# A one-core hybrid block: the context's decayed keys are made a pair ahead, and nine loads of the modulation's gate move behind the pairs

## The chip, the cores and the metric

The kernel runs on one core of one Trainium2 chip. TensorE (PE in the profile, with its weight loads as PEld), VectorE (DVE), ScalarE (ACT), GpSimd (POOL) and SyncE (SP, which here only starts loads) each work through a queue of their own in order, and wait for each other through semaphores. The metric is the time of one execution on the device in microseconds; less is better. Three runs of the kernel before gave 1631.05, 1633.28 and 1633.43 us, so the median is 1633.28 us.

## The reference

One block works on 256 tokens `x` of width 2048 and 256 context tokens `ctx`. Both are normalised and modulated by `c` and `c_ctx` through `w_ada`, and multiplied with one wide matrix `w_in`. Its columns feed a windowed attention, a gated linear recurrence (HGRN2) that runs in both directions, and two merge gates. The two branches go through `w_o_hgrn` and `w_o_attn`, are merged, and go through `w_out`; the result is scaled by a gate, which is the third part of the modulation, and added to `x`.

Two pieces matter here. The first is the state which the recurrence starts from. The context's tokens give it, with one forget gate f per token and channel, and keys k = 1 - f:

```python
def hgrn2_final_state(k, v, logf):
    G = jnp.cumsum(logf, axis=2)
    w = k.astype(jnp.float32) * jnp.exp(G[:, :, -1:, :] - G)
    return jnp.einsum('bhsk,bhsv->bhkv', w, v.astype(jnp.float32))

s_f = hgrn2_final_state(ck_f, cv_h, cg_f)
s_b = hgrn2_final_state(flip_t(ck_b), flip_t(cv_h), flip_t(cg_b))
```

So w, the decayed key of a context token, is its key times the product of all the forget gates behind it (ahead of it for the other direction). The second is the modulation's gate:

```python
mod = jax.nn.silu(c) @ w_ada[l] + b_ada[l]
shift, scale, gate = jnp.split(mod[:, None, :], 3, axis=-1)
h = h + gate * merge_and_project(...)
```

## The kernel before, in words

A matrix product in float32 is made of three products of rounded halves: each weight chunk (128 partitions x 1024 values, 512 KB, tile `raw`, four buffers) is loaded by SP's queue (L66), rounded on ACT to `wh` (L76), and the rest is left on DVE as `wl` (L77), three buffers each. PE then multiplies (L83, L84, L85, or L141 and L146 for columns whose two halves share a product). What PE does with one such chunk for 256 tokens is called a unit here; it is half a `STEP`.

The program has four stretches: the modulation with the first projections (to about 130 us), the forget gates and values of all heads (to about 570 us, gates written to DRAM as `F_dr`), the eight pairs of heads of the recurrence (570 to 1066 us), and then the output products with the attention between them.

In the third stretch `pair` is a generator. It issues some work of its own and yields how many `STEP`s of other work PE is to do before its next piece; `weave` takes that other work from `inputs`: output gates, merge gates, attention keys and values, and last the query columns of the next pair (L141, L146). PE's order is this order of writing. On DVE, ACT, POOL and SP the framework's scheduler sets the order when the kernel is built; `high_priority` marks the `wh` and `wl` work as urgent.

A pair's steps, by the names in the profile:

- The gates `F[0]` and `F[1]` (forward and backward; 512 columns for each of two heads, first the 256 tokens, then the 256 context tokens) come back from DRAM through POOL's queue (L1083). `load_forgets` for the next pair is called once four `STEP`s of other work are done. `F0` has two buffers, `F1` one.
- `E`, the decayed keys of the context: POOL writes the ones (L765, L766), DVE runs four scans (L770, L771) which multiply up the gates, and two operations (L774) make (f - 1) times the product. `E` lies in the pair's own tile `X2`.
- `tw`: eight transposes of `E` on PE (L899); ACT copies them to `wT` (L900). `to` (L993) turns the result of the pair before, and `sb` (L915) multiplies `wT` with the context's values.
- `copies` and `grow` (ACT L807 and L810, DVE L880): at levels 1, 2, 4, up to 64 the queries and keys are copied to slots and multiplied by gates; `al` (L834) are the products of those copies, in two sets. The first set has the levels up to 4, the second 8 to 64. Several slots are halves of `F0` and `F1` that are no longer needed: the context half of `F1` holds the queries of level 1, that of `F0` the keys of level 4.
- `own`, then `ob` (L973 to L975): the pair's output. `AT` and a state, both in `X2`, are read there.

Between these, `gates` makes the modulation's gate in 32 chunks: a load of `w_ada` into a `raw` buffer, and two operations on DVE that add it to `acc` (L194, L196). After each eight, four transposes `tqg` and a sum (L202, L204, L206) end a quarter. `with_gates` takes one chunk for every two `STEP`s of other work. What is left is run before `part_a`, the products with `w_o_hgrn` (four blocks of eight units each).

## Time and profile before

| What | Value |
|---|---|
| Median of three runs | 1633.28 us (1631.05 to 1633.43) |
| The profiled execution, its own time | 1626.34 us |
| Its span, first to last instruction | 1624.6 us |
| Mean granted clock of TensorE | 0.993 of full speed |
| Matmuls on PE | 10522, busy 98% of the span |
| DVE busy / ACT busy | 71% / 54% of the span |
| Data moved | 312.76 MB, mean 193 GB/s |

The profiled execution was 6.9 us shorter than the median. A row of a group gives the line, engine, operation, output and inputs, the count after the x, the time it was busy, the mean of one in ns, and then how long the engine had stood idle just before and on what. A row of waits gives who waited on whom, the total in us, how often, and the longest. A row of a stretch gives its bounds, its length, the busy time of each engine with the count of its instructions, the granted clock (1.00 is full speed), the share of the DMA engines and the GB/s. A row of the chain of work gives start, length, and what it was; rows of time order add the shape. A row of transfers gives the count, the KB of one, and the median us from issue to landing.

### The profile page before, as it was taken

What the parts mean: (1) busy time and instruction counts of PE and PEld (TensorE: products, weight loads), DVE (VectorE), ACT (ScalarE), POOL (GpSimd) and SP (SyncE); (2) the same over time, 40 slices, a digit from 0 to 9 for tenths busy, and PEclk for the clock granted to TensorE, in tenths of its full rate; (3) what the DMA queues carried; (4) which work ended last, traced back from release to release, by engine and by line L of the source; (5) the groups of instructions that cost most, each with busy time, mean ns of one, the idle gap of its engine ahead of it and who ended that gap; (6) DMA issues with size and microseconds to landing.
All of it is one profiled execution on the core that took longest, in us unless ns stands there. A gap on an engine that the chain in (4) does not pass through costs nothing.

```text
span 1624.6 us, 26679 instructions
## 1 busy us (share of the span) xinstructions
PE 1584.1 (98%) x10522; PEld 1335.9 (82%) x10522; DVE 1151.7 (71%) x1703; ACT 873.0 (54%) x1343; POOL 84.9 (5%) x183
## 2 busy tenths in 40 slices
PE   7999999999999999999999989999999999999998
PEld 4668888888899987888887877888888888878887
DVE  4449788888877777877878777555567767656764
ACT  4334465656543356645655656443457678744442
POOL 2000000000000010011010010000000000000000
PEclk9999999999999999999999999999999999999999
DMA  9994544444433477665766766455554445467662
GB/s 369 386 368 162 168 124 140 140 142 137 137 124 126 145 262 235 215 211 186 250 218 222 240 202 226 134 178 192 184 179 139 149 130 169 156 220 246 207 199 87
DMA packets 230013, 312.76 MB, mean 193 GB/s; under 512 B 10080, under 2 KB 145664, under 8 KB 228992
## 3 DMA queue, kind: packets, MB, share of 16 engines
q1 hardware_dynamic: 216800, 266.85, 50.3%
q0 software_dynamic: 12368, 43.11, 7.9%
q8 instruction: 82, 1.34, 0.3%
q10 hardware_dynamic: 720, 1.11, 0.2%
q14 instruction: 43, 0.35, 0.1%
HBM read 290.05 MB, written 20.98 MB: 191 GB/s over the span
## 4 chain that ended last, share of the span: by engine, by line
PE 87%; DVE 6%; DMA 3%; issue 2%; ACT 1%; POOL 0%; POOLq 0%; DVEq 0%; ACTq 0%
PE pj L83 13%; PE pj L84 13%; PE pj L85 13%; PE pj L141 6%; PE pj L630 5%; PE pm L630 5%; PE pj L146 3%; DMA raw<-in_w_ada_dram 3%; PE pj L633 3%; PE pm L633 3%; PE pj L415 2%; PE pa L311 2%; DVE wl L77 2%; PE pj L705 1%; PE pj L704 1%
## 5 line engine op out<-in xcount | busy, mean ns | idle before, releaser
L77 DVE TENSOR_TENSOR wl<-raw,wh 128x1024 fp32r<-128x1024 f32 x308 | 375.8, 1222 | 187.0 <-ACT wh L76 186.3
L76 ACT ACTIVATE wh<-raw 128x1024 fp32r<-128x1024 f32 x308 | 325.0, 1057 | 300.3 <-PE pj L85 218.5
L83 PE MATMUL pj<-wh,xHL 128*128 128x512 f32 (+1 forms) x832 | 324.4, 395 | 0.3 <-DVE hsum L156 0.3
L84 PE MATMUL pj<-wl,xHL 128*128 128x512 f32 (+1 forms) x832 | 323.2, 389 | 1.3 <-DVE wl L77 1.3
L85 PE MATMUL pj<-wh,xHL 128*128 128x512 f32 (+1 forms) x832 | 322.7, 388 | 0.0
L84 PEld LDWEIGHTS pj<-wl,xHL 128*128 128x128 f32 x832 | 157.8, 190 | 32.6 <-DVE wl L77 2.8
L85 PEld LDWEIGHTS pj<-wh,xHL 128*128 128x128 f32 x832 | 157.6, 189 | 32.4
L83 PEld LDWEIGHTS pj<-wh,xHL 128*128 128x128 f32 x832 | 157.9, 190 | 31.4 <-DVE hsum L156 0.7
L141 PE MATMUL pj<-xHL,wh 128*128 128x512 f32 x512 | 180.9, 395 | 0.0
L146 PE MATMUL pj<-xHL,wl 128*128 128x256 f32 x512 | 140.6, 285 | 0.0
L606 DVE TENSOR_TENSOR wl<-raw,wh 128x1024 fp32r<-128x1024 f32 x76 | 92.8, 1221 | 35.1 <-ACT wh L605 34.9
L605 ACT ACTIVATE wh<-raw 128x1024 fp32r<-128x1024 f32 x76 | 80.3, 1057 | 67.9 <-PE pj L630 22.3
L141 PEld LDWEIGHTS pj<-xHL,wh 128*128 128x128 f32 x512 | 95.0, 188 | 18.6
L605 ACT ACTIVATE wh<-T 128x1024 fp32r<-128x1024 f32 x57 | 60.5, 1061 | 80.9 <-PE pm L630 19.4
L84 PE MATMUL pj<-wl,bH 128*128 128x512 f32 x256 | 100.4, 393 | 0.4 <-DVE wl L77 0.4
L85 PE MATMUL pj<-wh,bL 128*128 128x512 f32 x256 | 99.4, 390 | 0.0
L146 PEld LDWEIGHTS pj<-xHL,wl 128*128 128x128 f32 x512 | 96.7, 189 | 2.5
L83 PE MATMUL pj<-wh,bH 128*128 128x512 f32 x256 | 91.8, 392 | 0.1
L606 DVE TENSOR_TENSOR wl<-T,wh 128x1024 fp32r<-128x1024 f32 x57 | 69.6, 1221 | 22.7 <-ACT wh L605 22.6
L880 DVE TENSOR_TENSOR A<-A,X 128x512 f32<-128x512 f32 x96 | 61.8, 685 | 7.6 <-ACT qk L810 2.4
L196 DVE SCALAR_TENSOR_TENSOR acc<-raw,cg,acc 128x512 f32<-128x512 f32 x60 | 44.8, 747 | 31.0 <-DMA raw<-in_w_ada_dram 30.9
L84 PEld LDWEIGHTS pj<-wl,bH 128*128 128x128 f32 x256 | 48.1, 188 | 10.8 <-DVE wl L77 1.0
(356 smaller groups left out, 2872.0 us busy)
## 6 DMA issues: line engine op xcount, KB each, us to landing
raw<-in_w_in_dram SPq DMA_DIRECT2D x300, 512.0 KB, 3.6
raw<-in_w_ada_dram SPq DMA_DIRECT2D x96, 512.0 KB, 7.6
raw<-in_w_o_hgrn_dram SPq DMA_DIRECT2D x32, 512.0 KB, 3.6
raw<-in_w_o_attn_dram SPq DMA_DIRECT2D x32, 512.0 KB, 4.2
F<-F POOLq DMA_DIRECT2D x29, 512.0 KB, 4.5
raw<-in_w_out_dram SPq DMA_DIRECT2D x28, 512.0 KB, 4.0
v<-vo POOLq DMA_DIRECT2D x8, 512.0 KB, 3.8
X<-in_x_dram SPq DMA_DIRECT2D x2, 1024.0 KB, 7.1
```

The lines of the kernel that those rows point to most:

```text
L76: act.activation(h[:, :n], raw[:, :n], AF.Copy)
L77: dve.tensor_tensor(lo[:, :n], raw[:, :n], h[:, :n].bitcast(F32), op=ALU.subtract)
L83: pe.matmul(o, s[0], m[0], start=first, stop=False)
L84: pe.matmul(o, s[0], m[1], start=False, stop=False)
L85: pe.matmul(o, s[1], m[0], start=False, stop=last)
L141: pe.matmul(banks[i].rearrange("p (a t) -> p a t", a=2), h[:, j, cs_], xHL[:, :, kt, :T], start=kt == 0, stop=kt == KT - 1)
L146: pe.matmul(banks[i][:, :T], lo[:, j, cs_], xH[:, kt, :T], start=False, stop=False)
L605: act.activation(h, src, AF.Copy)
L606: dve.tensor_tensor(lo, src, h.bitcast(F32), op=ALU.subtract)
L630: pe.matmul(m_[z].rearrange("p (z a t) -> p z a t", z=2, a=2), h[:, k, :], mv(k), start=fresh and k == 0, stop=False, skip_group_check=True)
L633: pe.matmul(pairs_of(m_[z][:, :T]), lo[:, k, :], mv(k)[:, 0], start=False, stop=k == 7, skip_group_check=True)
L880: dve.tensor_tensor(av, av, f.unsqueeze(3).to_broadcast([P, 2, n2, b]), op=ALU.mult)
```

## The change

The decayed keys are no longer made in `pair`. A new function `ctx_decay` makes them where `load_forgets` has issued the loads of the next pair's gates. It scans into a scratch tile `e` (tag `sm`, three buffers, shared with other work), and then overwrites the context half of `F[d]` with (f - 1) times `e`. The transposes read that half, and `E` in `X2` is gone. Since level 1's copy goes into the context half of `F1`, `copies(1)` moves behind the transposes, and the transposes move to the front of the pair: no other work is left between the pair before and them, and all 1.5 `STEP`s come behind. For the gate, a chunk is taken for every three `STEP`s and not two; the rest is taken in `part_a`, one chunk for every two units.

```diff
+    def ctx_decay(F):
+        rev = lambda a: bass.AP(a.tensor, a.offset + T - 2, [list(a.ap[0]), [-1, T - 1]])
+        for d in range(2):
+            e = base.tile([P, 512], F32, tag="sm", name="e", bufs=3).rearrange("p (h t) -> p h t", h=2)
+            for i in range(2):
+                if d == 0:
+                    pool.memset(e[:, i, T - 1: T], 1.0)
+                    dve.tensor_tensor_scan(rev(e[:, i, 0: T - 1]), rev(F[0][:, i, T + 1: 512]), zeros[:, : T - 1], 1.0,
+                                           ALU.mult, ALU.add)
+                else:
+                    pool.memset(e[:, i, 0:1], 1.0)
+                    dve.tensor_tensor_scan(e[:, i, 1:T], F[1][:, i, T: 511], zeros[:, : T - 1], 1.0, ALU.mult, ALU.add)
+            dve.scalar_tensor_tensor(F[d][:, :, T:], F[d][:, :, T:], -1.0, e, op0=ALU.add, op1=ALU.mult)
@@ pair
-        E = X2[:, :1024].rearrange("p (d h t) -> p d h t", d=2, h=2)
+        E = [F[d][:, :, T:] for d in range(2)]
-        for i in range(2):
-            pool.memset(E[:, 0, i, T - 1: T], 1.0)
-            pool.memset(E[:, 1, i, 0:1], 1.0)
-            fa = F[0][:, i, T + 1: 512]
-            ea = E[:, 0, i, 0: T - 1]
-            rev = lambda a: bass.AP(a.tensor, a.offset + T - 2, [list(a.ap[0]), [-1, T - 1]])
-            dve.tensor_tensor_scan(rev(ea), rev(fa), zeros[:, : T - 1], 1.0, ALU.mult, ALU.add)
-            dve.tensor_tensor_scan(E[:, 1, i, 1:T], F[1][:, i, T: 511], zeros[:, : T - 1], 1.0, ALU.mult, ALU.add)
-
-        for d in range(2):
-            dve.scalar_tensor_tensor(E[:, d], F[d][:, :, T:512], -1.0, E[:, d], op0=ALU.add, op1=ALU.mult)
...
-        copies(1)
-        yield 0.5
         wT = X2[:, 1024:].rearrange("p (a s) -> p a s", a=8)
         for d in range(2):
             tw = ps.tile([P, 512], F32, tag=alt(), name="tw")
             for i in range(2):
                 for s in range(2):
-                    pe.transpose(tw[:, (2 * i + s) * P: (2 * i + s + 1) * P], E[:, d, i, s * P: (s + 1) * P], ident)
+                    pe.transpose(tw[:, (2 * i + s) * P: (2 * i + s + 1) * P], E[d][:, i, s * P: (s + 1) * P], ident)
             act.activation(wT[:, 4 * d: 4 * d + 4, :], tw.rearrange("p (a b) -> p a b", a=4), AF.Copy)
-        yield 1.0
+        copies(1)
+        yield 1.5
@@ load_forgets
             nc.gpsimd.dma_start(F[d].rearrange("p i t -> p (i t)"), F_dr[d][n])
+        ctx_decay(F)
         return F
@@ with_gates
-            if count[0] >= 2 * STEP:
-                count[0] -= 2 * STEP
+            if count[0] >= 3 * STEP:
+                count[0] -= 3 * STEP
                 next(gate, None)
@@ part_a
-    run(gate)
...
-        by = proj_tok(w_oh, n * 512, b_st, range(2))
+        by = proj_tok_g(w_oh, n * 512, b_st, range(2))
+        for z in range(4):
+            take(gate, 1)
+            for _ in range(2):
+                next(by)
+        by = result(by)
...
     for n in range(4):
         part_a(n)
+    run(gate)
```

The order on three engines, as the kernels are built. First PE, from the end of one pair (`ob`) to the next pair's transposes (`tw`); before:

```order
L975 MATMUL ob<-so,A 128x128
L83 MATMUL pj<-wh,xHL 128x512
L84 MATMUL pj<-wl,xHL 128x512
L85 MATMUL pj<-wh,xHL 128x512
...
L899 MATMUL tw<-cs,X_6051 128x128 x8
```

and now:

```order
L979 MATMUL ob<-so,A 128x128
L902 MATMUL tw<-cs,F_5746 128x128 x4
L902 MATMUL tw<-cs,F_5747 128x128 x4
L83 MATMUL pj<-wh,xHL 128x512
L84 MATMUL pj<-wl,xHL 128x512
```

The unit of twelve matmuls that stood between the two stands behind the transposes now, which read the gates' tiles `F0` and `F1` of the pair.

Second DVE in the first pair, between its first set of `al` and its second; `copy_predicated` keeps a level from that first set, L880 (now L885) is `grow`, `wl` belongs to the units. Before:

```order
L880 TENSOR_TENSOR A<-A,X_5433 128x128x4 x2
L196 SCALAR_TENSOR_TENSOR acc<-raw,cg,acc 128x512
L849 COPY_PREDICATED X_5433<-mk,al 128x4x32
L515 TENSOR_TENSOR sgg<-pj,sgg 128x512
L196 SCALAR_TENSOR_TENSOR acc<-raw,cg,acc 128x512
L849 COPY_PREDICATED X_5433<-mk,al 128x4x32
L880 TENSOR_TENSOR A<-A,X_5433 128x64x8 x2
```

and now:

```order
L196 SCALAR_TENSOR_TENSOR acc<-raw,cg,acc 128x512
L761 SCALAR_TENSOR_TENSOR e<-F_5747,zero 128x255 x2
L854 COPY_PREDICATED X_5445<-mk,al 128x4x32
L885 TENSOR_TENSOR A<-A,X_5445 128x64x8 x2
L77 TENSOR_TENSOR wl<-raw,wh 128x1024
L762 SCALAR_TENSOR_TENSOR F_5747<-F_5747,e 128x2x256
```

The two scans (the listing calls them by the same operation as L762) and the product of the next pair's `F1` stand in this place now, ahead of `grow` and a `wl`.

Third SP, the loads at the end of the pairs and in `part_a`. Before:

```order
L66 DMA raw<-in_w_ada_dram 128x2x512
L66 DMA raw<-in_w_in_dram 128x2x512 x2
L66 DMA raw<-in_w_o_hgrn_dram 128x2x512 x32
L66 DMA raw<-in_w_in_dram 128x2x512 x8
```

and now:

```order
L66 DMA raw<-in_w_in_dram 128x2x512 x3
L66 DMA raw<-in_w_ada_dram 128x2x512 x2
L66 DMA raw<-in_w_o_hgrn_dram 128x2x512 x2
L66 DMA raw<-in_w_ada_dram 128x2x512
...
L66 DMA raw<-in_w_ada_dram 128x2x512
L66 DMA raw<-in_w_o_hgrn_dram 128x2x512 x14
```

Of the 32 loads of `w_ada` that the gate takes, all stood ahead of the first load of `w_o_hgrn`; now 23 do, and nine stand behind it, one after every two loads, up to the eighteenth.

## The prediction

> **What bounds the kernel now.** I read the page's first part, then who PE waited for in the stretch of the eight pairs, then that stretch's busy time and clock, and last the chain of work at two of the waits.

> ```profile
> span 1624.6 us, 26679 instructions
> PE 1584.1 (98%) x10522; PEld 1335.9 (82%) x10522; DVE 1151.7 (71%) x1703; ACT 873.0 (54%) x1343; POOL 84.9 (5%) x183
> ```

> PE is the bound: it is idle for 1624.6 - 1584.1 = 40.5 us of the whole. A change can win only from those, or from time in which PE runs at a lower clock. Stretches of the trace (bounds, length, PE, PEld, DVE, ACT and POOL busy, clock, DMA share, GB/s), the first the pairs, the next four around single stalls, the last `part_a`:

> ```profile
> 570.00:1060.00 490.00, 469.11 (x4344) 396.01 (x4343) 375.58 (x631) 284.72 (x527) 49.22 (x114) 0.98 0.66 216
> 587.00:594.00 7.00, 3.88 (x16) 3.15 (x16) 7.00 (x13) 3.04 (x5) 0.00 (x0) 0.76 0.62 223
> ...
> 826.00:833.00 7.00, 4.61 (x18) 3.45 (x17) 7.00 (x15) 2.74 (x5) 1.58 (x2) 0.76 0.66 221
> 885.00:895.00 10.00, 6.59 (x22) 5.54 (x22) 8.31 (x17) 2.98 (x6) 0.98 (x1) 0.66 0.46 152
> 947.00:956.00 9.00, 5.50 (x21) 4.05 (x20) 7.97 (x17) 4.86 (x8) 1.09 (x2) 0.81 0.62 206
> ...
> 1066.00:1163.00 97.00, 97.00 (x450) 80.53 (x449) 49.68 (x50) 39.80 (x48) 2.34 (x4) 1.00 0.60 196
> ```

> In the pairs PE is idle for 490.0 - 469.1 = 20.9 us. What it waited for there:

> ```profile
> PE tw L899 <- DVE X L774: 16.7, 8, 3.4
> PE pj L84 <- DVE wl L77: 1.3, 1, 1.3
> ```

> The transposes of `E` waiting for DVE's last operation on `E` are 16.7 of the 20.9 us, over eight pairs. And a long stall costs twice: after four of them the clock falls (0.76, 0.76, 0.66 and 0.81 as means of those stretches). The lost clock is (1 - 0.76) x 7 = 1.7, 1.7, 3.4 and 1.7 us, a little of it inside the idle itself. The chain at the second pair shows why DVE is late (start, length, what):

> ```profile
> 643.98 0.60 DVE acc L196
> ...
> 644.64 1.22 DVE wl L77
> 645.86 0.33 DVE hsum L156
> ...
> 646.52 0.60 DVE X L770
> 647.12 0.58 DVE X L771
> ...
> 648.78 0.68 DVE X L774
> 649.50 1.26 PE tw L899 x8
> 650.76 0.23 PE pj L83
> ```

> Four scans and two products run in a row behind the gate's `acc`, a `wl` and `hsum`, and PE has one unit of twelve matmuls at 0.23 us, 2.7 us, as cover.

> **The change part by part.**

> *The transposes' wait, pairs 2 to 8.* The next pair's `F1` is issued when the first `al` set has read the old one:

> ```profile
> 611.50 0.46 PE L834 MATMUL al<-qk 128*32 128x32 f32 x32
> 612.79 0.53 POOL L1083 DMA_DIRECT2D F<-F  x1 [29.50 <-ACT wh L76]
> F<-F POOLq DMA_DIRECT2D x15, 512.0 KB, 5.7
> ```

> It lands at about 612.8 + 5.7 = 618.5, while the pair it is for wants its transposes as soon as `ob` has ended, at 643.9 (just ahead of the chain quoted above). That leaves 25 us for three DVE operations; `F0` has two buffers and comes earlier still. So `E` is there, and without the first pair's stall (3.1 us: 587.9 to 591.0) the gain is 16.7 - 3.1 = 13.6 us. Its bounds are 13.6 and, should DVE be late again, the rivals below.

> *The clock behind these stalls.* Without the first pair, 1.7 + 3.4 + 1.7 = 6.8 us by the rows above, some of it in the idle already counted. I take 6; the bounds are 4 and 7.

> [...]

> *The first pair gets worse.* Here nothing is made ahead: the gates `F0` land just before.

> ```profile
> 584.94 0.25 PE pj L141
> ...
> 587.45 1.26 DVE X L770 x2
> ...
> 590.35 0.61 DVE X L774
> 591.01 1.97 PE tw L899 x8
> ```

> DVE keeps this order (one `acc` of 0.4 us moves behind), so `E` is ready at about 590.5 as before. But PE has no unit left between 585.2 and the transposes; it idles 5.3 us, not 3.1, and the unit comes after. That is 2.7 - 0.5, with a little more at the lower clock: +2.5 us, bounds +2 and +4.

> *DVE's work moves into the pair before.*

> ```profile
> L77 DVE TENSOR_TENSOR wl<-raw,wh 128x1024 fp32r<-128x1024 f32 x123 | 149.9, 1221 | 63.9 <-ACT wh L76 63.4
> L196 DVE SCALAR_TENSOR_TENSOR acc<-raw,cg,acc 128x512 f32<-128x512 f32 x60 | 44.8, 747 | 31.0 <-DMA raw<-in_w_ada_dram 30.9
> L770 DVE TENSOR_TENSOR_SCAN X<-F,zero 128x255 f32<-128x255 f32 x16 | 10.7, 672 | 0.1
> L774 DVE SCALAR_TENSOR_TENSOR X<-F,X 128x512 f32<-128x512 f32 x16 | 10.4, 677 | 0.0
> ```

> Counts and durations stay: per direction two scans and a product, 2 x 0.67 + 0.68 = 2.0 us. The `F0` half now stands near the start of a pair, where 4.0 us have gone; that is room. The `F1` half stands between the first and the second `al` set, in front of `grow` and a `wl`. By the order and these durations DVE gets there some four to six microseconds after the first set's start (an estimate), and `F1` lands 612.8 + 5.7 - 611.5 = 7.0 us after it. So DVE waits 1 to 3 us there, with everything behind it in its queue: the rest of `grow`, from which the second set's copies are made, and the units' `wl`. What they have to spare in the first pair:

> ```profile
> 627.30 0.62 ACT L810 ACTIVATE so<-A 128x512 f32<-128x512 f32 x1
> 630.98 0.65 PE L834 MATMUL al<-so,acc 128*32 128x64 f32 x32
> ```

> The copy ends at 627.9, PE reads it at 631.0: 3.1 us (the least of the eight; the others have up to 6). Against it: 2.0 us of work, about 2 of waiting, 2.6 because PE comes earlier; for it: 4.0 - 2.0 at the pair's start, and the gate. A chunk costs DVE two operations of 0.75 us, and 30.9 us of waiting for its load over 32 chunks, so about 2.5 us; a pair had four and gets under three, so some 3 us. Nearly even: 6.6 against 5, on 3.1 to 6 us to spare. I take 0.4 us for each of seven pairs, +3; the bounds are 0 and 10.

> POOL's queue gets the same 32 small fills as before, ahead of loads that land long before their use: nothing. `copies(1)` moves behind the transposes on ACT, 1 us of PE, while the first `al` set is six units away: nothing.

> *The gate in `part_a`.* There PE never waits (97.00 of 97 us), and DVE, busy 49.7 us, has room for nine chunks' 13.5 us. What is scarce is the four `raw` buffers. Now three loads come in two units, 5.5 us, so a buffer's turn is 4/3 of that, 7.3 us, and must hold the landing, `wh` and `wl`:

> ```profile
> raw<-in_w_o_hgrn_dram SPq DMA_DIRECT2D x24, 512.0 KB, 3.6
> raw<-in_w_ada_dram SPq DMA_DIRECT2D x32, 512.0 KB, 4.3
> raw<-in_w_ada_dram SPq DMA_DIRECT2D x96, 512.0 KB, 7.6
> L76 ACT ACTIVATE wh<-raw 128x1024 fp32r<-128x1024 f32 x128 | 134.8, 1056 | 105.2 <-PE pj L85 61.1 <-PE pj L141 17.5 <-issue 11.2
> GB/s 369 386 368 162 168 124 140 140 142 137 137 124 126 145 262 235 215 211 186 250 218 222 240 202 226 134 178 192 184 179 139 149 130 169 156 220 246 207 199 87
> ```

> The rows are: `part_a` (3.6 us at 196 GB/s), the gate in the pairs (4.3 at 216), and the whole run, most of it in the first slices (7.6 at 369 to 386). With half as much again `part_a` wants about 290 GB/s, so I estimate a landing of 5 to 6 us. 5.3 + 1.06 + 1.22 = 7.6 us, 0.3 over the turn, over eighteen units (49 us): +2; with DVE's queue waiting for a chunk's load now and then I take +3. The bounds are 0 (4.3 us landing, 6.6 in all) and +18 (7.6 us landing, 9.9 in all: 36% of 49 us).

> *The sum.* -13.6 - 6 + 2.5 + 3 + 3 = -11 us. The profiled execution would come from 1626.3 to about 1615. The median of the runs is 6.9 us above that execution, and I take the same difference for the change: 1633.3 - 11 = **1622 us**.

> **The rivals.**

> *DVE becomes the bound inside the pairs.* The stall at `tw` goes, and comes back at the second `al` set or as a wait for `wl`, since DVE waits for `F1` in its queue. For it: DVE was busy 375.6 of 490 us, and its queue is in order. Against it: PE waited for `wl` once, 1.3 us, though `acc` kept DVE waiting 21 times. At 1.5 us more for each of seven pairs, +10, the gain is nearly gone: -1, so 1632; at half of that 1627.

> *The gate's loads starve `part_a`* (the side on which it gets slower). If with nine more loads the transfers land as late as at the start, 7.6 us, a buffer's turn is 9.9 us and PE waits 18 us there: -11 - 3 + 18 = +4, so 1637. It decides from a landing of about 7 us, where the loss is the 14 us won elsewhere. For it: 290 GB/s is three quarters of the highest slice. Against it: the pairs' 216 GB/s cost only 0.7 us of landing more than `part_a`'s 196.

> *The keys are not ready after all* for one reason or another, and the transposes wait without their unit of cover: 16.7 + 7 x 2.7 = 36 us of stalls, 1650 and more. The 25 us speak against it.

> **How the numbers follow.** A measurement of this kernel tells about 0.2%, 3.3 us, from no change. I give my forecast 0.67, DVE as the bound 0.18, the starved `part_a` 0.08, keys not ready 0.04; 0.03 is left for more than the forecast allows. Faster by more than 3.3 us are the forecast, the last case and a third of the second: 0.67 + 0.03 + 0.07 = 0.77. No change is the rest of the second and a part of the third, 0.13. Slower is the remaining 0.10. The forecast's own range goes from all terms at their good ends (-13.6 - 7 + 2 = -19, 1614) to 1628. The range on record is 1612 to 1632: below, small waits of the other 4.2 us may go too; above, it takes in most of the second case.

> **What would show it.** PE's wait at `tw` should be one entry of about 5 us, in the first pair, and its clock low only behind that one. PE's idle time in the pairs should be 10 to 13 us. Any new wait should name `al` on ACT or DVE, or `wl`. DVE should wait for `F` about seven times, 1 to 3 us each, and for `w_ada` less than 30.9 us. In `part_a` the landing should be under 6 us and PE idle under 5. I am wrong if the transposes wait in later pairs, if PE's new waits in the pairs exceed 10 us, or if `part_a` grows by more than 5.

## The result and the profile after

The changed kernel takes 1618.84 us, the kernel before 1633.36 us (medians of four runs each): a ratio of 0.9911, 95% interval 0.989 to 0.9932. Measured again (the run after_again below) it takes 1619.75 us against 1628.36 us, a ratio of 0.9947, 0.9933 to 0.9961. Two executions, one of after_again at 1737.60 us and one of own_cover_late at 3178.83 us, lie far above all others and are left out of the medians and ratios here. The change is faster in both comparisons. Its own time is nearly the same in both; the kernel before was 5 us slower in the first than in the three later jobs, where its 47 runs have medians of 1627.2 to 1628.4 us. Three of the four runs of the kernel before in the first comparison are those that were on record before the change was timed, so the second is the better one; why the kernel before was slower then stays open. The gain is 14.5 us by the first comparison and 8.6 us by the second.

The profiled execution took 1616.09 us. The first part of its page:

```profile
span 1614.3 us, 26652 instructions
PE 1578.8 (98%) x10522; PEld 1331.8 (82%) x10522; DVE 1152.6 (71%) x1703; ACT 869.5 (54%) x1343; POOL 82.3 (5%) x183
```

The work is the same in number. The pairs and the stage behind them, as stretches with the busy time of PE, PEld, DVE, ACT and POOL, the clock, the DMA share and GB/s:

```profile
570.00:1060.00 490.00, 477.01 (x4415) 404.06 (x4414) 372.20 (x625) 285.90 (x539) 50.13 (x115) 0.99 0.66 213
1060.00:1160.00 100.00, 98.24 (x442) 79.52 (x441) 62.24 (x69) 40.05 (x42) 0.58 (x1) 1.00 0.69 223
```

PE is idle for 490.0 - 477.0 = 13.0 us in the pairs, where it was 20.9. The clock lost there, which is PE's busy time in each microsecond times the missing share of the clock, is 2.0 us in sum, where it was 7.5. Behind the pairs PE is idle for 1.8 us, where it never was. What PE waited for in the pairs (us in all, times, the longest):

```profile
PE pj L84 <- DVE wl L77: 3.3, 5, 1.4
PE tw L902 <- DVE F L762: 5.4, 1, 5.4
PE ob L979 <- DVE X L965: 3.3, 2, 1.9
PE pj L146 <- DVE wl L77: 0.8, 2, 0.5
```

The transposes wait once, in the first pair, and the clock falls only behind that wait:

```profile
585.00:598.00 13.00, 7.56 (x30) 6.18 (x29) 11.25 (x21) 6.73 (x12) 0.25 (x4) 0.74 0.56 194
```

The waits for `wl` and at `ob` have grown: 7.4 us together, where there were 1.3 for `wl` and 1.0 for `X` at `ob`. DVE's own waits in the pairs say where they come from:

```profile
DVE acc L196 <- DMA raw<-in_w_ada_dram: 29.6, 15, 5.5
DVE e L761 <- DMA F<-F: 5.7, 6, 1.6
```

DVE waits 5.7 us for the gates in six pairs, and, with nine chunks fewer, still 29.6 us for the loads of `w_ada` (30.9 before). The chain of waits ahead of the first and longer of the two waits at `ob` (1.9 us) shows one such load:

```profile
690.72 7.72 DMA raw<-in_w_ada_dram
...
698.46 0.76 DVE acc L196
...
699.91 1.22 DVE wl L77
701.13 0.79 DVE X L965 x3
...
701.96 0.49 PE ob L979 x2
```

DVE takes its queue in order here. It stands at the add for 5.49 us, until the load has landed, starts it at 698.46 us, and then PE's `wl` (699.91) and the operations on `X` (701.05) come one after another.

In the stage behind the pairs the loads of `w_o_hgrn` land later than before (3.6 us there), and ACT, which never waited for them, does now:

```profile
raw<-in_w_o_hgrn_dram SPq DMA_DIRECT2D x24, 512.0 KB, 4.7
```

```profile
ACT wh L76 <- DMA raw<-in_w_o_hgrn_dram: 23.6, 11, 4.0
```

The pairs' last `ob` starts 15.4 us earlier (1066.1 to 1050.7), and the attention behind `part_a` starts about 10 us earlier. So the pairs won some 15 us in the two profiled executions, and the stage behind them gave 4 to 5 back.

### The profile page after: what moved, and what is told of

Read it like the earlier page. It is cut to its first block, busy times and chain, and to the rows that moved or that the text cites. A ratio compares the mean times of both kernels' runs of the same rounds, so it can differ in the third digit from the quotient of the medians.

```text
span 1614.3 us, 26652 instructions
## 1 busy us (share of the span) xinstructions
PE 1578.8 (98%) x10522; PEld 1331.8 (82%) x10522; DVE 1152.6 (71%) x1703; ACT 869.5 (54%) x1343; POOL 82.3 (5%) x183
## 4 chain that ended last, share of the span: by engine, by line
PE 87%; DMA 5%; DVE 4%; issue 2%; ACT 1%; SPq 0%; POOL 0%; POOLq 0%; DVEq 0%; ACTq 0%
PE pj L84 13%; PE pj L83 13%; PE pj L85 13%; PE pj L141 6%; PE pj L630 5%; PE pm L630 5%; PE pj L146 3%; PE pj L633 3%; PE pm L633 3%; DMA raw<-in_w_ada_dram 2%; DVE wl L77 2%; PE pj L415 2%; PE pa L311 2%; DMA F<-F 1%; PE pj L705 1%
## 5 line engine op out<-in xcount | busy, mean ns | idle before, releaser
L77 DVE TENSOR_TENSOR wl<-raw,wh 128x1024 fp32r<-128x1024 f32 x308 | 375.4, 1221 | 167.4 <-ACT wh L76 166.5
L76 ACT ACTIVATE wh<-raw 128x1024 fp32r<-128x1024 f32 x308 | 324.6, 1056 | 287.5 <-PE pj L85 180.5
L84 PE MATMUL pj<-wl,xHL 128*128 128x512 f32 (+1 forms) x832 | 322.1, 387 | 3.3 <-DVE wl L77 3.3
L83 PE MATMUL pj<-wh,xHL 128*128 128x512 f32 (+1 forms) x832 | 322.2, 392 | 0.0
L85 PE MATMUL pj<-wh,xHL 128*128 128x512 f32 (+1 forms) x832 | 321.2, 386 | 0.0
L84 PEld LDWEIGHTS pj<-wl,xHL 128*128 128x128 f32 x832 | 156.8, 188 | 36.0 <-DVE wl L77 6.7
L85 PEld LDWEIGHTS pj<-wh,xHL 128*128 128x128 f32 x832 | 156.6, 188 | 31.8
L83 PEld LDWEIGHTS pj<-wh,xHL 128*128 128x128 f32 x832 | 156.7, 188 | 30.6 <-ACT sg L211 0.4
L141 PE MATMUL pj<-xHL,wh 128*128 128x512 f32 x512 | 180.9, 395 | 0.0
L141 PEld LDWEIGHTS pj<-xHL,wh 128*128 128x128 f32 x512 | 95.0, 188 | 18.6
L84 PE MATMUL pj<-wl,bH 128*128 128x512 f32 x256 | 100.9, 395 | 2.2 <-DVE wl L77 2.2
L85 PE MATMUL pj<-wh,bL 128*128 128x512 f32 x256 | 99.3, 390 | 0.0
L83 PE MATMUL pj<-wh,bH 128*128 128x512 f32 x256 | 92.0, 393 | 0.1
L606 DVE TENSOR_TENSOR wl<-T,wh 128x1024 fp32r<-128x1024 f32 x57 | 69.6, 1221 | 22.9 <-ACT wh L605 22.9
L196 DVE SCALAR_TENSOR_TENSOR acc<-raw,cg,acc 128x512 f32<-128x512 f32 x60 | 44.9, 748 | 32.9 <-DMA raw<-in_w_ada_dram 32.4
L885 DVE TENSOR_TENSOR A<-A,X 128x512 f32<-128x512 f32 x96 | 61.8, 685 | 4.8 <-ACT so L815 2.4
L84 PEld LDWEIGHTS pj<-wl,bH 128*128 128x128 f32 x256 | 48.1, 188 | 13.8 <-DVE wl L77 4.0
## 6 DMA issues: line engine op xcount, KB each, us to landing
raw<-in_w_in_dram SPq DMA_DIRECT2D x300, 512.0 KB, 3.7
raw<-in_w_ada_dram SPq DMA_DIRECT2D x96, 512.0 KB, 7.8
raw<-in_w_o_hgrn_dram SPq DMA_DIRECT2D x32, 512.0 KB, 4.6
raw<-in_w_o_attn_dram SPq DMA_DIRECT2D x32, 512.0 KB, 4.2
F<-F POOLq DMA_DIRECT2D x29, 512.0 KB, 4.8
raw<-in_w_out_dram SPq DMA_DIRECT2D x28, 512.0 KB, 4.3
v<-vo POOLq DMA_DIRECT2D x8, 512.0 KB, 4.0
```

Source lines behind the costliest of these rows:

```text
L76: act.activation(h[:, :n], raw[:, :n], AF.Copy)
L77: dve.tensor_tensor(lo[:, :n], raw[:, :n], h[:, :n].bitcast(F32), op=ALU.subtract)
L83: pe.matmul(o, s[0], m[0], start=first, stop=False)
L84: pe.matmul(o, s[0], m[1], start=False, stop=False)
L85: pe.matmul(o, s[1], m[0], start=False, stop=last)
L141: pe.matmul(banks[i].rearrange("p (a t) -> p a t", a=2), h[:, j, cs_], xHL[:, :, kt, :T], start=kt == 0, stop=kt == KT - 1)
```

## The experiments

Three jobs of four kernels ran on three chips, and in each job the kernel before ran beside them; ratios are to that. They and their intervals are worked out over the single runs and are not quite the quotients of the two medians.

| Run | Median, us | Kernel before, us | Ratio, 95% interval |
|---|---|---|---|
| keys_only | 1636.53 | 1627.79 | 1.0057 (1.0043 to 1.0071) |
| gate_only | 1620.85 | 1627.79 | 0.9962 (0.9946 to 0.9978) |
| cover_all | 1616.08 | 1627.79 | 0.9929 (0.9915 to 0.9943) |
| gate_all_late | 1646.56 | 1627.79 | 1.0123 (1.0104 to 1.0141) |
| after_again | 1619.75 | 1628.36 | 0.9947 (0.9933 to 0.9961) |
| gate_only_again | 1621.36 | 1628.36 | 0.9949 (0.9937 to 0.9962) |
| keys_unread | 1622.22 | 1628.36 | 0.9967 (0.9956 to 0.9978) |
| own_buffers | 1614.66 | 1628.36 | 0.9916 (0.9903 to 0.9929) |
| own_cover | 1615.27 | 1627.18 | 0.9924 (0.9909 to 0.9939) |
| gate_own | 1616.19 | 1627.18 | 0.9929 (0.9912 to 0.9946) |
| fill_before | 1629.08 | 1627.18 | 1.0012 (0.9997 to 1.0026) |
| own_cover_late | 1612.09 | 1627.18 | 0.9899 (0.988 to 0.9918) |

### The keys alone

Against the changed kernel, the gate is put back to where it was:

```diff
-            if count[0] >= 3 * STEP:
-                count[0] -= 3 * STEP
+            if count[0] >= 2 * STEP:
+                count[0] -= 2 * STEP
...
+    run(gate)
...
-        by = proj_tok_g(w_oh, n * 512, b_st, range(2))
-        for z in range(4):
-            take(gate, 1)
-            ...
+        by = proj_tok(w_oh, n * 512, b_st, range(2))
```

> The keys a pair ahead and the transposes first, but the gate's chunks all taken in the pairs as before. My theory (the gain is the stall at the transposes and its clock): the wait at the transposes is about 5.4 us, once, in the first pair, as in the changed kernel, and part_a has no idle time; DVE has nine more chunks in the pairs, so the other waits of PE there grow from 8 us to 10 to 16 us. Time -9 to -14 us against the kernel before, 1620 to 1624 us. Rival (the gate's move is what frees DVE): PE's new waits in the pairs eat the gain, -5 us or less, 1628 us or more.

It was 8.7 us slower than the kernel before, 1636.53 us where I expected 1620 to 1624. The transposes did what was predicted, but PE waits for `wl` instead; its waits in the pairs:

```profile
PE pj L84 <- DVE wl L77: 19.5, 6, 5.3
PE tw L902 <- DVE F L762: 5.8, 1, 5.8
```

The chain of waits at one of the six, in the second pair:

```profile
671.75 7.40 DMA raw<-in_w_ada_dram
...
679.18 0.75 DVE acc L196
...
681.00 1.19 DVE A L885 x2
682.19 1.18 DVE e L761 x2
683.37 1.13 DVE wl L77
...
684.54 0.80 PE pj L84
```

DVE waits for a chunk of `w_ada`, and behind it now stand `grow`, the scans of the next pair's `F1` and only then the `wl`. It is so at all six. In order of time, for the fourth pair (the time in brackets is what the engine stood idle just before):

```profile
808.35 0.75 DVE L196 SCALAR_TENSOR_TENSOR acc<-raw,cg,acc 128x512 f32<-128x512 f32 x1 [4.98 <-DMA raw<-in_w_ada_dram]
...
814.90 0.80 PE L84 MATMUL pj<-wl,xHL 128*128 128x512 f32 x1 [5.26 <-DVE wl L77]
```

| The six waits in `keys_only` | 1 | 2 | 3 | 4 | 5 | 6 |
|---|---|---|---|---|---|---|
| DVE at the load of `w_ada`, us | 1.93 | 2.54 | 4.98 | 3.30 | 4.53 | 1.61 |
| PE at the `wl` behind it, us | 1.62 | 3.60 | 5.26 | 2.77 | 4.82 | 1.40 |

PE lost 28.9 us to idling and 10.1 us of clock between 560 and 1200, where the kernel before lost 20.9 and 7.5.

### The gate alone

The kernel before, with `with_gates` and `part_a` as in the change, and the keys as they were:

```diff
-            if count[0] >= 2 * STEP:
-                count[0] -= 2 * STEP
+            if count[0] >= 3 * STEP:
+                count[0] -= 3 * STEP
...
-    run(gate)
...
-        by = proj_tok(w_oh, n * 512, b_st, range(2))
+        by = proj_tok_g(w_oh, n * 512, b_st, range(2))
+        for z in range(4):
+            take(gate, 1)
+            for _ in range(2):
+                next(by)
+        by = result(by)
...
+    run(gate)
```

> The kernel before with only the gate's chunks moved. My theory: the eight waits at the transposes stay, 12 to 17 us in all, with two to four falls of the clock behind them, since four scans and two products still stand in a row; part_a pays 4 us. Time 1631 to 1637 us, no gain. Rival (DVE's load with the gate is why the keys come late): the waits at the transposes fall under 9 us and the time is 1625 us or less.

It was 6.9 us faster, where I expected no gain. Its waits from 560 to 1100 us (the three at L84 lie behind the pairs):

```profile
PE tw L899 <- DVE X L774: 12.0, 9, 2.7
PE pj L146 <- DVE wl L77: 2.2, 1, 2.2
PE pj L84 <- DVE wl L77: 1.3, 3, 0.5
```

Which waits got shorter shows in DVE's order. A star marks a pair in which one of the gate's adds to `acc` started in the 8 us ahead of the transposes:

| Wait at `tw` in the pair, us | 2 | 3 | 5 | 6 | 7 | 8 |
|---|---|---|---|---|---|---|
| Kernel before | 2.64* | 0 | 2.39* | 3.41* | 3.50* | 1.60* |
| gate_only | 1.20 | 1.50* | 2.11* | 0.58 | 0.58 | 3.27* |

The fourth pair, where PE has 11 us of other work ahead of its transposes, waits in neither. With fewer chunks, fewer pairs have a chunk in front of the scans. gate_only_again and gate_own (below) show the same: 1.3 to 3.9 us with an add there, 0.6 to 1.2 without. That the adds make the difference is read from this order; no run changed it alone.

So the part that I had written down as a cost is a gain by itself, and the part that I had written down as the gain is a loss by itself. If the two added up, both together would be 1.8 us slower than before; they are 8.6 us faster in the second comparison. To see what the keys are worth beside the moved gate, the change and the gate alone were run side by side.

> The change itself, once more, beside the kernel with the gate's move alone on the same chip. If the two parts help each other (keys ahead are cheap only once the gate has moved), it is 2 to 6 us faster than the gate's move alone, because the waits at the transposes, 12.0 us there, are replaced by some 5.4 us in the first pair and 4.2 us of waits for wl. If the gate's move is all that there is, the two are within 1 us.

> The kernel before with the gate's move alone, measured again on the same chip as the whole change. 5 to 9 us below the kernel before, as in the first measurement (ratio 0.996), with waits at the transposes of about 12 us and a clock that hardly falls; the whole change is 2 to 6 us below it if the keys ahead are worth anything.

The medians are 1619.75 and 1621.36 us, between my two cases, and the intervals of the ratios are nearly the same: no difference that can be told. What PE waited for in the change here, from 560 to 1100 us:

```profile
PE pj L84 <- DVE wl L77: 6.1, 9, 2.1
PE tw L902 <- DVE F L762: 5.4, 1, 5.4
PE ob L979 <- DVE X L965: 2.4, 2, 1.5
PE pj L146 <- DVE wl L77: 0.9, 2, 0.6
```

That is 14.8 us, against 17.4 for the gate alone in the same job, of which 13.4 are waits at the transposes. The keys ahead replaced most of the waits at the transposes with others. The idle time and the clock of the two profiled executions differ by more than the medians do (the profile of the gate alone is of its longest run, 1625.22 us, with 8.0 us of lost clock), so the medians decide here.

### Is it DVE's wait for the load?

The keys alone, but the gate's sums in the pairs read a resident tile; the loads of `w_ada` are still made and nothing reads them, so that the modulation's gate is left out of the result.

```diff
-        wr = wload(w_ada, k0 * P, 2, (4096 + 512 * g,), 512)[1][:, 0]
+        wload(w_ada, k0 * P, 2, (4096 + 512 * g,), 512)
+        wr = xH[:, k0: k0 + 2, :].bitcast(F32)
```

> The keys made ahead, with the gate's place as in the kernel before, but the gate's sums in the pairs read a tile that lies in the core's memory already instead of the loaded w_ada; the loads are still issued and nothing reads them (so the modulation's gate is wrong). DVE has the same instructions in the same order and only its wait for these loads is gone. If that wait is what held the scans and the wl behind it, PE's waits for wl fall from 19.5 us to under 5 and the time from 1636 to about 1614 to 1618. If it is the amount of DVE's work in that place, or the wait for F, the waits for wl stay over 12 us and the time over 1630.

```profile
PE pj L84 <- DVE wl L77: 6.9, 8, 1.6
PE al L840 <- ACT so L816: 5.6, 2, 3.3
PE tw L903 <- DVE F L763: 5.4, 1, 5.4
```

From a ratio of 1.0057 to 0.9967: the waits for `wl` fell from 19.5 to 6.9 us, and some 14 us of time went with them. I had allowed 5 us, and 1614 to 1618 us for the time, which is 1622.22; 5.6 us appeared at `al`.

The loads and the number of DVE's instructions are the same, but not the order, against what I expected. Adds that need not wait were placed elsewhere by the scheduler: of the gate's 64 operations sixteen run from 127 to 170 us, far ahead of the pairs, and the others in three bursts, from 715 to 739, 823 to 866 and 940 to 981 us. The first, second, fourth and sixth pair have none. So this run takes away the wait and moves the work as well, and can't say alone which of the two counts. The amount does count: the fifth and seventh pair, with a burst of twice the adds and no wait, take 61.2 and 59.1 us from one `tw` to the next, where they took 58.7 and 56.5 in `keys_only`. One thing else changed: nothing reads these `raw` buffers any more, and what that is worth to the ring of four was not measured.

That the wait at the load is what made the keys dear rests on the six pairs of numbers above. The change fits in: DVE still stands at loads of `w_ada` there, but none of these waits over 1 us has the scans behind it and then a `wl` for which PE waits. Its two long ones, 5.5 and 5.3 us, stand ahead of `ob` and cost PE 1.9 and 1.4 us.

### All of the gate behind the pairs

The change with no chunk in the pairs and one per unit in `part_a`, 32 in all:

```diff
-            if count[0] >= 3 * STEP:
-                count[0] -= 3 * STEP
-                next(gate, None)
...
-            take(gate, 1)
             for _ in range(2):
+                take(gate, 1)
                 next(by)
```

> The changed kernel with all 32 chunks of the gate in part_a, one for every unit. My theory (the four raw buffers set the pace of part_a): a buffer's turn there is 5.5 us and must hold a landing of 4.7 us or more, wh and wl, 7 us together, so part_a grows by 15 to 30 us; the pairs lose up to 8 us of small waits: 1625 to 1640 us. Rival (the loads aren't the bound, DVE's order is): part_a grows by less than 6 us over the changed kernel's, 1612 to 1618 us.

```profile
560.00:1040.00 480.00, 467.56 (x4403) 399.19 (x4402) 344.97 (x572) 282.17 (x519) 48.17 (x113) 1.00 0.59 192
1040.00:1180.00 140.00, 121.11 (x495) 90.42 (x494) 95.79 (x125) 45.93 (x62) 3.71 (x6) 0.94 0.74 248
```

It took 1646.56 us, more than the 1625 to 1640 that I gave. The pairs, with only the first adds of the gate at their end, still idle 12.4 us. From 1040 us on PE now idles 18.9 us and the clock falls (0.94 as the mean of that stretch), and ACT waits 65.5 us for the loads of `w_o_hgrn`, which land after 5.0 us. The rival of a starved `part_a` is real; with nine chunks it was not reached.

### The buffers in `part_a`

The change, with the late gate loads in two buffers that lie idle there:

```diff
-        wr = wload(w_ada, k0 * P, 2, (4096 + 512 * g,), 512)[1][:, 0]
+        if gate_pool[0] is None:
+            wr = wload(w_ada, k0 * P, 2, (4096 + 512 * g,), 512)[1][:, 0]
+        else:
+            gate_pool[1] ^= 1
+            own = gate_pool[0].tile([P, 2, 512], F32, tag=("qk", "so")[gate_pool[1]], name="own_raw")
+            ...
+            wr = own
```

> The whole change, but the nine gate loads that went to the stage behind the pairs land in two buffers of their own instead of taking turns in the four raw buffers of the projection's weights. If the shared turns are what costs there (1.8 us of idle PE and a landing of 4.7 us instead of 3.6), PE's idle time in that stage goes to about 0 and the kernel gains 1 to 3 us over the whole change. If it is the memory's rate, the idle time stays near 1.8 us and the time is the same.

```profile
raw<-in_w_o_hgrn_dram SPq DMA_DIRECT2D x23, 512.0 KB, 4.7
...
own_raw<-in_w_ada_dram SPq DMA_DIRECT2D x9, 512.0 KB, 5.0
```

```profile
1060.00:1160.00 100.00, 99.37 (x451) 81.45 (x451) 65.17 (x75) 40.12 (x42) 0.59 (x1) 1.00 0.69 234
```

The landing stays at 4.7 us, so the turns of the buffers don't set it; over these runs it goes with the traffic (3.6 us at 196 GB/s, 4.7 at 223 and 234, 5.0 at 248). But ACT no longer waits for a load there (23.6 us in the change's first profile, no entry here), and PE idles 0.6 us, where after_again has 2.7. So it was the turns of the four buffers that turned the later landing into a stall. The gain in the medians is 5.1 us, more than those 2 us; gate_own is 11.0 us below the kernel before of its job and gate_only_again 7.0 below its own, 4 us between them. What the rest is, the profiled executions don't show.

### What the half clock is worth

The kernel before, with 24 transposes that nothing uses ahead of `tw`'s, in the four pairs where the clock fell behind the stall:

```diff
+            if h0 in (0, 8, 10, 12) and d == 0:
+                idle = ps.tile([P, 512], F32, tag="tp", name="idle")
+                for q in range(24):
+                    pe.transpose(idle[:, (q % 4) * P: (q % 4 + 1) * P], ident, ident)
```

> The kernel before, with 24 transposes of the unit matrix, some 2.6 us, ahead of the waiting transposes in the four pairs whose stall was over 3 us. They compute nothing that is used and fill time in which PE waits anyway. If the half clock behind these stalls costs what the records show (7.5 us of lost clock in the pairs), the clock stays at full speed there and the kernel is 4 to 7 us faster. If the clock behind a stall costs nothing, because DVE is what comes last there too, the time is the same; if the fillers come late into their own way, it is slower.

```profile
560.00:1060.00 500.00, 482.72 (x4513) 410.87 (x4512) 381.82 (x637) 287.67 (x532) 51.95 (x117) 1.00 0.66 215
```

```profile
PE pj L84 <- DVE wl L77: 7.6, 3, 4.3
PE tw L903 <- DVE X L774: 7.0, 6, 2.4
```

The clock was kept: 1.7 us lost where it was 7.5. But the kernel got no faster. The 5.8 us came back as waits for `wl`, which grew from 1.3 to 7.6 us. The chain at the longest, 4.3 us, is again a load in DVE's queue:

```profile
909.56 7.16 DMA raw<-in_w_ada_dram
...
917.41 0.29 DVE X L849
...
921.17 1.13 DVE wl L77
922.34 0.50 PE pj L84
```

PE's faster work only brought it sooner to a `wl` that DVE could not make yet. The 1.6 us won in the first pair were still there in the fourth, whose `ob` starts at 818.9 and not 821.1 us; the waits for `wl` in the fifth and sixth, 2.4 and 4.3 us, ate them and what was won there. So the second of my cases came, DVE last there too, and not the gain of 4 to 7 us.

### The cover, and the place of the scans

One unit back ahead of the transposes, in every pair, in the change:

```diff
+        yield 0.5                   # ahead of tw's transposes
...
-        yield 1.5
+        yield 1.0
```

> The changed kernel with one unit back in front of the transposes in every pair. My theory: only the first pair feels it, its wait falls from 5.4 us to about 3 us and the time is 2 to 3 us under the changed kernel's, 1616 us; in the other pairs nothing waits at the transposes either way. Rival (the place of the transposes matters for ACT and the banks behind): new waits in the other pairs, the same time or more than the changed kernel.

The first pair's wait fell from 5.4 to 2.7 us, and the waits for `wl` up to 1100 us rose from 5.1 to 8.3. The ratio is 0.9929 against 0.9947 for the change on another chip; the intervals overlap. With the own buffers as well, and beside it everything but the keys:

> The whole change with two things mended: the gate loads of the stage behind the pairs land in two buffers of their own, and one unit of matmuls stands ahead of the transposes again in every pair, as in the kernel before. If both gains add up (6 us for the buffers, about 3 us for the unit, which shortened the first pair's stall from 5.4 to 2.7 us), it is at 1611 to 1613 us, 9 us below the whole change. If PE's idle time only moves to the next wait for wl, it stays at 1614 to 1616, where the own buffers alone are.

> The kernel before with the gate's move alone, and the gate loads of the stage behind the pairs in two buffers of their own: everything but the keys ahead. If the keys ahead are worth nothing once the gate has moved, as the two kernels of the last job say (1620.9 against 1621.4 us), it is within 2 us of the whole change with own buffers (1614.7 us there), and 3 us or more behind the one that has the covering unit as well only if keys and cover together are worth something. If the keys are worth their stalls, it stays at 1618 or more.

```profile
PE pj L84 <- DVE wl L77: 7.3, 7, 3.2
PE tw L912 <- DVE F L771: 2.7, 1, 2.7
...
PE pj L146 <- DVE wl L77: 2.0, 2, 1.7
```

1615.27 against 1616.19 us. These waits are those of own_cover: the gains did not add up, and keys with cover are not worth 3 us either. Last, the scans for the next pair at the end of a pair's other work, so that DVE doesn't reach them before the gates have landed:

```diff
-        ctx_decay(F)                # in load_forgets
...
+            ctx_decay(F)            # behind a pair's other work
...
+        ctx_decay(res[0])           # for the first pair
```

> The first kernel of this job with the next pair's scans emitted at the end of a pair's other work instead of where the gates' loads are issued, so that DVE should not stand waiting for F. If DVE's wait for F (7 to 9 us over six pairs) holds up wl and so PE, the waits for wl fall by 2 to 5 us and the time by as much. If what is queued there has time to spare, the time is within 1.5 us of the first kernel; if the scans now stand ahead of the next pair's own chain, PE waits more at ob, al or tw and it is slower.

```profile
PE pj L84 <- DVE wl L77: 5.4, 6, 1.4
PE tw L912 <- DVE F L771: 3.4, 1, 3.4
PE al L970 <- ACT X L860: 1.6, 1, 1.6
PE ob L989 <- DVE X L975: 1.3, 1, 1.3
PE pj L146 <- DVE wl L77: 0.9, 2, 0.6
```

1612.09 us, the best of all, 15 us below the kernel before of its job. DVE's wait for `F` in the pairs fell from 8.9 us in own_cover to 0.6, and the waits for `wl` fell from 9.3 to 6.3 us; the time fell by 3.2. Against gate_own it is 4.1 us, so here the keys ahead earn something; but the intervals of the ratios touch, and one pair of kernels is no more than a sign.

## Why the prediction was right, and where it was not

The time came out at 1618.84 and 1619.75 us, where 1622 was predicted, and the range held both. That the number is so near is in part luck, since two of the terms have their sign from the wrong part of the change. The terms, in their order:

- *The transposes' wait, -13.6.* Right as a fact: no pair but the first waits at `tw`. The eight waits that made it up lay in six of the eight pairs, the third and fourth had none. Wrong as a gain: 5.1 us of it came back as waits for `wl` and at `ob` (7.4 - 2.3), and beside the moved gate alone the keys gain nothing that can be told (1619.75 against 1621.36).
- *The clock, -6.* By the records 7.5 - 2.0 = 5.5 us. Filling the stalls of the kernel before saved as much clock and, by the end, no time. The term doesn't stand by itself while DVE sets the end.
- *The first pair, +2.5.* PE idles 5.4 us there, as predicted (5.3), and its `sb` starts 3.4 us later (601.5 to 604.9), within the bounds of 2 to 4.
- *DVE's work in the pair before, +3.* DVE waits for `F` six times, 5.7 us in all and at most 1.6, near what was said. But this is the step that failed. I let the gate's smaller share give back some 3 us of DVE's time and set it against the scans as two amounts that nearly cancel. The runs show that the place counts more than the amount: whether DVE stands at a load of `w_ada` with the scans and a `wl` behind it. With the gate's old share the keys cost 19.5 us of waits for `wl`, and the kernel gets slower than before; my bounds of 0 to 10 were for the smaller share, but nothing in the term says that all hangs on it. The waits for `w_ada` need not fall with the number of chunks either (30.9 to 29.6 us in the first pair of profiles, 24.0 in after_again). That the new waits would name `al` was wrong as well; they are at `wl` and `ob`.
- *The gate in `part_a`, +3.* Right in its mechanism. The landing rose to 4.7 us (5.3 estimated), PE idles 1.8 us by the first profile and 2.7 by the second, ACT waits for loads, and own buffers take that away.
- *The sum.* PE's idle time in the pairs was to be 10 to 13 us, and is 13.0. But I booked the gain to the keys and a net cost to the gate. Alone, the keys cost 8.7 us and the gate's move wins 6.9. The start of the sum, 1633.3 us, did not come again either (1628.4 in the second comparison). And in the chances a third of 0.18 is 0.06, not 0.07.

Of the rivals, DVE as the bound inside the pairs is what the keys alone turned into, at a higher price than I gave it (1636.5 us, not 1632). The starved `part_a` is what all 32 chunks there give. Neither came with both parts in place.

The gate's move alone shortens the waits at the transposes (16.7 to 12.0 and 13.4 us) in the pairs that no longer have a chunk ahead of the scans; what of that is the add's own time and what the wait for its load was not taken apart.

## What to carry to other kernels

A wait that ends at an engine can be only where a load shows, further up in that engine's queue (all six long waits for `wl` in keys_only are): follow the chain past the last operation, and before moving work ahead ask which load the engine will stand at with that work behind it. Price the parts of a change together with what stands in front of them in the queue; here one part lost 9 us alone, the other won 7 alone, and the sum of both said nothing about the pair. Keeping the clock up need not win its time: fill_before lost 5.8 us less of it, its waits for `wl` grew by 6.3 us, and it took 1629.08 us against 1627.18. And when an edit takes away a wait, compare the built order before reading the result: the scheduler may have moved the work too.

## What the runs showed of the hardware

The clock did not fall behind every stall. In the kernel before, a wait of 2.64 us that ends at 649.5 left it at full speed, while behind one of 1.84 us that ends at 828.6 it stood at half (0.50 from 829.32 to 832.73 us). The four microseconds behind each:

```profile
649.50:653.50 4.00, 4.00 (x21) 3.32 (x22) 4.00 (x9) 1.20 (x2) 0.00 (x0) 1.00 0.04 14
828.60:832.60 4.00, 3.45 (x13) 2.83 (x14) 4.00 (x9) 1.19 (x2) 0.54 (x1) 0.59 0.44 139
```

Over the pairs and the stage behind them in thirteen profiled executions (all but that of gate_all_late), all 14 stalls of 3.1 us and more were followed by half clock, and 15 of the 28 between 1.7 and 3.0 us. Counted from where the clock falls, the time at half clock was 3.4 us in 19 of the 29 and 6.8 us in the other ten.
